# A decoder step on TensorE: the moving rows stored in two halves, every second token in the other half

## The chip, the core and the metric

The kernel runs on one core of one Trainium2 chip. The metric is the time in microseconds (us) that the device takes for one execution of the program; lower is better. Traces come from the hardware profiler, for one execution.

## The reference

One inference step of a hybrid decoder layer for two groups of requests that share all weights: a prompt of 256 tokens and 8 single-token samples, together 264 token columns. All data is float32, the model width is 2048. In short:

```python
def layer(x):
    proj = rms_norm(x, g_mix) @ w_in            # 2048 x 6688: q, k, v | z, xBC | dt
    attn = sliding_window_attention(q, k, v)    # 16 heads of 64, window 128, sinks
    ssd  = mamba2(z, conv4(xBC), dt)            # 32 heads of 64, state 128
    x = x + concat([attn, ssd]) @ w_out         # 3072 x 2048
    q = rms_norm(rms_norm(x, g_cross) @ w_cq)   # 4 heads of 128
    k, v = rms_norm(h @ w_ck), h @ w_cv         # h = rms_norm(memory, g_mem), 256 memory tokens
    x = x + softmax(q k / sqrt(128)) v @ w_co   # 512 x 2048
    u = conv3(rms_norm(x, g_ffn) @ w_up)        # 2048 x 11264
    return x + (silu(gate) * val) @ w_down      # 5632 x 2048
```

The samples use cached keys, values, memory and convolution rows in place of those of the prompt, and the step also returns the new caches and states.

## The kernel before, in words

Everything is kept transposed: features on the 128 partitions, tokens along the row. A matrix product takes a 128x128 block of weights as the stationary operand and a row of 264 tokens (256 prompt, 8 samples) as the moving one, and adds 264 output columns into a PSUM bank.

Precision is held by a split. Each float32 number is stored as two numbers of the type fp32r, a high part (the value rounded) and a low part (the rest). `weights` (L76) loads 1024 columns of weights at a time into `wraw`, ScalarE writes the high part `whi` (L89), VectorE the low part `wlo` (L90). `split` (L94) does the same for the tokens: ScalarE writes the high part, VectorE the low part (L97 without a gain, L98 and L99 with one). `mm3` (L104) then makes a block's product out of three: high weights with high tokens (L105), high weights with low tokens (L106), low weights with high tokens (L107). `proj` (L109) loops over weight units, the two or four output blocks and the blocks of the sum.

The split tokens lie in tiles that `rows` (L67) makes: 8 rows of a pitch of 320 numbers, of which 264 are used, each with token t at place t:

```python
PITCH = 320
    def rows(tag, name):
        return apool.tile([128, 8, PITCH], F32R, tag=tag, name=name, bufs=4)[:, :, :T]
```

These tiles are `A` (xh, xl: input of the layer, written by `x_hi` L165 and `x_lo` L169 in the opening), `Y` (yh, yl: the gated state-space output), `AT` (ath, atl: the attention output), `X1` (x1h, x1l), `OH` and `OL` (ohl: the cross-attention output), `X2` (x2h, x2l: the FFN's input) and `H` (hh, hl: the FFN's hidden rows). Some are written in two parts, the 256 prompt columns by one pair of instructions and the 8 sample columns by another.

In order of time: an opening in which the input and the first weights arrive and 192 products run (`first_k`, L242, to about 30 us); the input projection with convolutions, attention and the state-space scan between its products (to about 360 us); the output projection (to about 499 us); the cross-attention, in which memory keys (`keys`, L1159) and values (`v_pair`, L1280) are made the other way round, with the memory rows as stationary operand and the weights as the moving one, 512 columns for keys and 256 for values (to about 605 us); the FFN, 44 hidden blocks in six groups, up-projections of a group alternating with down-projections of the one before (to the end). The order of instructions on each engine is set by the tile framework's scheduler, with priorities and `issue_after` marks; the opening is ordered by hand. All weight loads are issued from SyncE's queue, and a load waits until VectorE has finished with the buffer. GpSimd issues some state loads and stores and does small elementwise work.

Of the kernel before, what the change touches and what calls it, by code (L numbers as in the profile page):

```python
# [48 lines left out]
def hybrid_decoder_step_kernel(ctx: ExitStack, tc: tile.TileContext, I, O):  # L49
# [17 lines left out]
    def rows(tag, name):  # L67
        return apool.tile([128, 8, PITCH], F32R, tag=tag, name=name, bufs=4)[:, :, :T]

# [24 lines left out]
    def split(hi, lo, x, g=None):  # L94

        if g is None:
            return S.copy(out=hi, in_=x), V.tensor_tensor(out=lo, in0=x, in1=hi.bitcast(F32), op=ALU.subtract)  # L97
        return (S.activation(out=hi, in_=x, func=AF.Copy, scale=g),  # L98
                V.scalar_tensor_tensor(out=lo, in0=x, scalar=g, in1=hi.bitcast(F32), op0=ALU.mult, op1=ALU.subtract))  # L99
# [9 lines left out]
    def proj(units, acts, evac, n=T, nb=2, tag="mm"):  # L109

        outs = [psum(t) for t in (tag if isinstance(tag, list) else [tag] * nb)]
        for ui, (src, act) in enumerate(zip(units, acts)):
            parts = src if isinstance(src, list) else weights(src)
            for pi, (wh, wl) in enumerate(parts):
                wh = wh.rearrange("p (k c) -> p k c", c=128 * nb)
                wl = wl.rearrange("p (k c) -> p k c", c=128 * nb)
                nk = wh.shape[1]
                for m in range(nb):
                    for k in range(nk):
                        kk = pi * nk + k  # L120
                        ah, al = act(8 * ui + kk) if callable(act) else (act[0][:, kk, :n], act[1][:, kk, :n])
                        last = mm3(outs[m][:, :n], wh[:, k, m * 128:(m + 1) * 128], wl[:, k, m * 128:(m + 1) * 128],
                            ah, al,
                            ui == 0 and kk == 0, ui == len(units) - 1 and kk == nk * len(parts) - 1)
                if ui == 0:
                    marks["part"] = last
        for m in range(nb):
            with tc.high_priority():
                evac(m, outs[m][:, :n])
# [35 lines left out]
    def x_hi(k):  # L165
        x, g = x_of(k)
        return S.activation(out=A[k // 8][0][:, k % 8, :], in_=x, func=AF.Copy, scale=g)

    def x_lo(k):  # L169
        x, g = x_of(k)  # L170
        return V.scalar_tensor_tensor(out=A[k // 8][1][:, k % 8, :], in0=x, scalar=g, in1=A[k // 8][0][:, k % 8, :].bitcast(F32),
                                      op0=ALU.mult, op1=ALU.subtract)
# [27 lines left out]
    with tc.manual_schedule(engines={mybir.EngineType.SP, mybir.EngineType.PE, mybir.EngineType.Activation, mybir.EngineType.DVE}):  # L200
# [41 lines left out]
        def first_k(k, i):  # L242

            for x in range(2 - i):
                for c in range(4):
                    PE.matmul(first[c][:, :T], pre[k // 2][i][:, k % 2, c * 128:(c + 1) * 128], A[k // 8][x][:, k % 8, :],  # L246
                              start=k + i + x == 0, stop=k == KB - 1 and i == 1)
# [698 lines left out]
    def z_pair(i):  # L946
# [9 lines left out]
        for m in range(2):  # L956
            k = 2 * i + m
            y = y2[:, m, :]
            sumsq(accy[:, :TP], y, k == 0, TP, V)
            split(Y[k // 8][0][:, k % 8, :TP], Y[k // 8][1][:, k % 8, :TP], y, gssd[:, k:k + 1])  # L960

    def gate_sample():
# [13 lines left out]
        for h in range(2):  # L976
            split(Y[h][0][:, :, TP:T], Y[h][1][:, :, TP:T], ysam[:, 8 * h:8 * h + 8, :])

# [32 lines left out]
    with tc.high_priority():  # L1011
        for j in (0, 4):
            split(AT[0][:, j:j + 4, :], AT[1][:, j:j + 4, :], attn[:, j:j + 4, :])
    w_out = I["w_out"]
# [66 lines left out]
    for i in range(8):  # L1081
        def ev(m, pm, i=i):
            k = 2 * i + m
            x = res[k // 4][:, k % 4, :]
            t = small.tile([128, T], F32, tag="raw", name="raw")
            V.tensor_tensor(out=t, in0=pm, in1=ry, op=ALU.mult)
            V.tensor_tensor(out=x, in0=t, in1=x, op=ALU.add)
            marks["x1"] = split(X1[k // 8][0][:, k % 8, :], X1[k // 8][1][:, k % 8, :], x, pc("g_cross", k))
        proj([w_out[8 + 2 * i], w_out[9 + 2 * i]], Y, ev, tag="t" if i % 2 else "mm")
# [69 lines left out]
    def keys():  # L1159
        pk = [psum("mm") for _ in range(2)]  # L1160
        for u in range(4):
            for pi, (wh, wl) in enumerate(weights(I["w_ck"][u])):
                wh, wl = (w.rearrange("p (k c) -> p k c", c=512) for w in (wh, wl))
                for k in range(2):
                    kk = 4 * u + 2 * pi + k
                    mhi, mlo = mem_hl(kk)
                    for c in range(2):
                        cs = slice(c * 128, c * 128 + 128)
                        mm3(pk[c], mhi[:, cs], mlo[:, cs], wh[:, k, :], wl[:, k, :], kk == 0, kk == KB - 1)
        ks = xp.tile([128, 2, 4], F32, name="ks")  # L1170
# [65 lines left out]
    def sample_out():  # L1236
# [14 lines left out]
        for q in range(2):  # L1251
            x = p[:, 0:128].rearrange("p (j c) -> p j c", j=4)[:, :, 4 * q:4 * q + 4].rearrange("p j m -> p m j")
            cs = slice(TP + 4 * q, TP + 4 * q + 4)
            split(OH[:, :, cs], OL[:, :, cs], x)
# [25 lines left out]
    def v_pair(i):  # L1280
        pv = [psum("mm") for _ in range(2)]
        for u in range(2):
            parts = [w.rearrange("p (k c) -> p k c", c=256) for hl in weights(I["w_cv"][2 * i + u]) for w in hl]
            nk = parts[0].shape[1]
            for k in range(8):
                wh, wl = parts[2 * (k // nk)], parts[2 * (k // nk) + 1]
                mhi, mlo = mem_hl(8 * u + k)
                for c in range(2):
                    cs = slice(c * 128, c * 128 + 128)
                    mm3(pv[c][:, 0:256], mhi[:, cs], mlo[:, cs], wh[:, k % nk, :], wl[:, k % nk, :],  # L1290
                        u + k == 0, u == 1 and k == 7)
# [3 lines left out]
    def out_head(h):  # L1295
# [4 lines left out]
        with tc.high_priority():  # L1300
            return split(OH[:, h, :TP], OL[:, h, :TP], o[:, 0:256])

# [22 lines left out]
    OHL = rows("A", "ohl")  # L1325
    OH, OL = OHL[:, 0:4, :], OHL[:, 4:8, :]
    lg = sample_logits()
# [19 lines left out]
    def x2_ev(k, pm):  # L1347
        x = res[k // 4][:, k % 4, :]
        V.tensor_tensor(out=x, in0=pm, in1=x, op=ALU.add)
        split(X2[k // 8][0][:, k % 8, :], X2[k // 8][1][:, k % 8, :], x, pc("g_ffn", k))  # L1350


    outs = [psum(t) for t in ("mm", "mm", "t", "t")]
    for pi, (wh, wl) in enumerate(weights(I["w_co"][0])):
        wh, wl = (w.rearrange("p (k c) -> p k c", c=512) for w in (wh, wl))
        for k in range(2):
            h = 2 * pi + k
            for m in range(4):
                ms = slice(m * 128, m * 128 + 128)
                mm3(outs[m][:, :T], wh[:, k, ms], wl[:, k, ms], OH[:, h, :], OL[:, h, :], h == 0, h == 3)  # L1360
    for m in range(4):
# [63 lines left out]
    def up(g):  # L1425
        H = (rows("A", f"hh{g}"), rows("A", f"hl{g}"))
        n = len(groups[g])
        for ii, i in enumerate(groups[g]):
# [27 lines left out]
            V.tensor_tensor(out=cs[1], in0=cs[0], in1=cs[1], op=ALU.mult)  # L1456
            split(H[0][:, ii, :TP], H[1][:, ii, :TP], cs[1])
        b0 = groups[g][0]
# [8 lines left out]
        V.tensor_tensor(out=sc[1], in0=sc[0], in1=sc[1], op=ALU.mult)  # L1467
        split(H[0][:, 0:n, TP:T], H[1][:, 0:n, TP:T], sc[1])
        return H
# [53 lines left out]
def _pack(np, x):  # L1523
# [129 lines left out]
```

## Time and profile before

| what | value |
|---|---|
| median of 3 runs | 1376.23 us (1375.93 to 1378.35) |
| profiled execution | 1375.38 us, span 1373.6 us |
| TensorE busy | 1368.6 us, 100% of the span, 11412 products and transposes |
| VectorE, ScalarE, GpSimd busy | 1045.0, 769.5, 90.8 us |
| HBM traffic | 216 GB/s over the span |
| granted TensorE clock | full in all slices |

The span runs from the first to the last instruction; the execution's own time has some 1.8 us around it. A TensorE row's duration reaches from its start to its modelled end and overlaps that of the next products, so the distance between two starts, and not the duration, says how long TensorE is held. "128*128 128x264" in such a row is the shape of the weights and of the moving operand; "x2h,whi" are the moving and the stationary tile, or the other way round where the name sorts so. Weight loads have rows of their own (PEld) and overlap the products.

### The profile page before, as it was taken

Reading aid. Unit: us, or ns where it says so; the run is one execution under the profiler, and the core shown is the slowest. Engines: PE = TensorE matmul, PEld = TensorE weight load, DVE = VectorE, ACT = ScalarE, POOL = GpSimd, SP = SyncE. Lnnn points to the kernel's source line nnn. Section 1 sums busy time; section 2 is a strip of 40 time slices with the busy share of each in tenths; the row PEclk is TensorE's granted clock in tenths of the full one; section 3 lists DMA queues with packets and bytes.
Section 4 is the critical chain, followed back from the end, with each engine's and each line's share of the span. In section 5 each row is a group of like instructions: output and inputs, shape, how many; then the busy total and the mean of one; then the engine's idle time right before and its main releaser. Section 6 shows DMA issues by size and latency. Waiting matters only on the chain.

```text
span 1373.6 us, 28651 instructions
## 1 busy us (share of the span) xinstructions
PE 1368.6 (100%) x11412; PEld 1347.2 (98%) x11412; DVE 1045.0 (76%) x1797; ACT 769.5 (56%) x1253; POOL 90.8 (7%) x284
## 2 busy tenths in 40 slices
PE   9999999999999999999999999999999999999998
PEld 9999999999999999899999999999999999999998
DVE  8979899999987774488777765776577657765655
ACT  7667776855546545475566644554455446544532
POOL 0000101111100000002110000000000000000000
PEclk9999999999999999999999999999999999999999
DMA  7954588667786576675676765676567556655554
GB/s 304 329 158 150 174 281 261 196 212 229 243 262 210 182 244 221 259 268 190 197 248 220 251 219 179 221 255 216 184 215 246 196 187 198 198 180 185 194 185 137
DMA packets 88326, 298.31 MB, mean 217 GB/s; under 512 B 11905, under 2 KB 17025, under 8 KB 87681
## 3 DMA queue, kind: packets, MB, share of 16 engines
q1 hardware_dynamic: 82688, 277.61, 60.9%
q0 software_dynamic: 5504, 18.88, 4.2%
q8 instruction: 89, 1.46, 0.4%
q14 instruction: 45, 0.36, 0.1%
HBM read 280.77 MB, written 16.23 MB: 216 GB/s over the span
## 4 chain that ended last, share of the span: by engine, by line
PE 100%; DVE 0%; ACT 0%; issue 0%
PE mm L107 21%; PE mm L105 21%; PE mm L106 21%; PE t L107 10%; PE t L106 10%; PE t L105 10%; PE t L246 1%; PE t L284 1%; PE x L866 1%; PE mm L246 0%; PE s L246 0%; PE x L284 0%; PE s L875 0%; PE t L569 0%; PE x L1198 0%; PE x L1242 0%
## 5 line engine op out<-in xcount | busy, mean ns | idle before, releaser
L89 ACT CAST whi<-wraw 128x1024 fp32r<-128x1024 f32 x440 | 460.4, 1048 | 531.1 <-PE mm L106 279.2
L90 DVE TENSOR_TENSOR wlo<-wraw,whi 128x1024 fp32r<-128x1024 f32 x440 | 541.9, 1233 | 218.3 <-ACT whi L89 212.0
L107 PE MATMUL t<-x2h,wlo 128*128 128x264 f32 x704 | 198.6, 282 | 0.0
L106 PE MATMUL t<-x2l,whi 128*128 128x264 f32 x704 | 198.4, 282 | 0.0
L105 PE MATMUL t<-x2h,whi 128*128 128x264 f32 x704 | 198.4, 282 | 0.0
L106 PE MATMUL mm<-hl,whi 128*128 128x264 f32 x704 | 197.6, 282 | 0.0
L107 PE MATMUL mm<-hh,wlo 128*128 128x264 f32 x704 | 197.3, 282 | 0.0
L105 PE MATMUL mm<-hh,whi 128*128 128x264 f32 x704 | 195.7, 282 | 0.0
L105 PE MATMUL mm<-x2h,whi 128*128 128x264 f32 x672 | 189.4, 282 | 0.0
L106 PE MATMUL mm<-x2l,whi 128*128 128x264 f32 x672 | 189.4, 282 | 0.0
L107 PE MATMUL mm<-x2h,wlo 128*128 128x264 f32 x672 | 189.4, 282 | 0.0
L107 PE MATMUL mm<-xh,wlo 128*128 128x264 f32 x576 | 164.4, 287 | 0.0
L106 PE MATMUL mm<-xl,whi 128*128 128x264 f32 x576 | 163.3, 284 | 0.0
L105 PE MATMUL mm<-xh,whi 128*128 128x264 f32 x576 | 163.3, 285 | 0.0
L107 PEld LDWEIGHTS t<-x2h,wlo 128*128 128x128 f32 x704 | 131.9, 187 | 0.0
L105 PEld LDWEIGHTS t<-x2h,whi 128*128 128x128 f32 x704 | 131.9, 187 | 0.0
L106 PEld LDWEIGHTS t<-x2l,whi 128*128 128x128 f32 x704 | 131.9, 187 | 0.0
L106 PEld LDWEIGHTS mm<-hl,whi 128*128 128x128 f32 x704 | 131.9, 187 | 0.0
L107 PEld LDWEIGHTS mm<-hh,wlo 128*128 128x128 f32 x704 | 131.7, 187 | 0.0
L105 PEld LDWEIGHTS mm<-hh,whi 128*128 128x128 f32 x704 | 130.8, 187 | 0.0
L105 PEld LDWEIGHTS mm<-x2h,whi 128*128 128x128 f32 x672 | 125.9, 187 | 0.0
L106 PEld LDWEIGHTS mm<-x2l,whi 128*128 128x128 f32 x672 | 125.9, 187 | 0.0
(522 smaller groups left out, 2933.4 us busy)
## 6 DMA issues: line engine op xcount, KB each, us to landing
wraw<-in_w_up_dram SPq DMA_DIRECT2D x176, 512.0 KB, 4.1
wraw<-in_w_in_dram SPq DMA_DIRECT2D x96, 512.0 KB, 4.4
wraw<-in_w_dn_dram SPq DMA_DIRECT2D x88, 512.0 KB, 4.2
wraw<-in_w_out_dram SPq DMA_DIRECT2D x48, 512.0 KB, 4.5
h<-in_h_dram POOLq DMA_DIRECT2D x32, 256.0 KB, 4.7
hn<-in_h_dram SPq DMA_DIRECT2D x16, 512.0 KB, 4.9
out_state_s_dram<-hn POOLq DMA_DIRECT2D x16, 512.0 KB, 3.3
late<-dram_la SPq DMA_DIRECT2D x8, 512.0 KB, 6.8
```

The lines of the kernel that those rows point to most:

```text
L89: highs.append(S.copy(out=hi, in_=x))
L90: lows.append(V.tensor_tensor(out=lo, in0=x, in1=hi.bitcast(F32), op=ALU.subtract))
L105: PE.matmul(out, wh, xh, start=start, stop=False)
L106: PE.matmul(out, wh, xl, start=False, stop=False)
L107: return PE.matmul(out, wl, xh, start=False, stop=stop)
L246: PE.matmul(first[c][:, :T], pre[k // 2][i][:, k % 2, c * 128:(c + 1) * 128], A[k // 8][x][:, k % 8, :], start=k + i + x == 0, stop=k == K ...
L284: return PE.transpose(out, in_, cst[0:k, C_ID:C_ID + k])
L866: PE.matmul(st, Bn[:, c, g, :], sts[c].rearrange("p h q -> p (h q)"), start=True, stop=True)
```

## The change

The rows of split tokens keep their pitch and their 264 places, but token t = 2b + a now lies at place 132 a + b: even tokens fill the first half, odd tokens the second. The view that `rows` returns has the two dimensions b (132, step 1) and a (2, step 132), so whoever goes through it in order meets the tokens in their natural order, reading or writing the two halves in turn. `split`, `x_hi` and `x_lo` write through this view (their input is viewed as pairs), the products read through it, and the output columns in PSUM are in natural order as before. Prompt columns are the pairs 0 to 127, sample columns the pairs 128 to 131.

The key and value weights, which are the moving operand of the memory's products, are permuted on the host (`apart`): in each group of 512 (keys) or 256 (values) columns the even columns come first. The products read them through the same kind of view, halves 256 and 128 numbers apart. No instruction, transfer or wait is added or taken away. The products of the attention's own keys (kh, kl), the plain float32 products and the transposes stay as they are.

```diff
     def rows(tag, name):
-        return apool.tile([128, 8, PITCH], F32R, tag=tag, name=name, bufs=4)[:, :, :T]
+        return apool.tile([128, 8, PITCH], F32R, tag=tag, name=name, bufs=4)[:, :, :T].rearrange("p k (a b) -> p k b a", a=2)
+
+    PROMPT, SAMPLES = slice(0, TP // 2), slice(TP // 2, T // 2)
+
+    def pairs(x):
+
+        if len(x.shape) == 2:
+            return x.rearrange("p (b a) -> p b a", a=2)
+        return x.rearrange("p k (b a) -> p k b a", a=2)
...
     def split(hi, lo, x, g=None):
 
+        if len(hi.shape) > len(x.shape):
+            x = pairs(x)
...
-                        ah, al = act(8 * ui + kk) if callable(act) else (act[0][:, kk, :n], act[1][:, kk, :n])
+                        ah, al = act[0][:, kk], act[1][:, kk]
...
-        return S.activation(out=A[k // 8][0][:, k % 8, :], in_=x, func=AF.Copy, scale=g)
+        return S.activation(out=A[k // 8][0][:, k % 8], in_=pairs(x), func=AF.Copy, scale=g)
...
-            split(Y[k // 8][0][:, k % 8, :TP], Y[k // 8][1][:, k % 8, :TP], y, gssd[:, k:k + 1])
+            split(Y[k // 8][0][:, k % 8, PROMPT], Y[k // 8][1][:, k % 8, PROMPT], y, gssd[:, k:k + 1])
...
-                wh, wl = (w.rearrange("p (k c) -> p k c", c=512) for w in (wh, wl))
+                wh, wl = (w.rearrange("p (k a b) -> p k b a", k=2, a=2) for w in (wh, wl))
...
-            parts = [w.rearrange("p (k c) -> p k c", c=256) for hl in weights(I["w_cv"][2 * i + u]) for w in hl]
+            parts = [w.rearrange("p (k a b) -> p k b a", a=2, b=128) for hl in weights(I["w_cv"][2 * i + u]) for w in hl]
...
-            split(H[0][:, ii, :TP], H[1][:, ii, :TP], cs[1])
+            split(H[0][:, ii, PROMPT], H[1][:, ii, PROMPT], cs[1])
...
+    def apart(w, c):
+
+        return w.reshape(w.shape[0], -1, c // 2, 2).swapaxes(2, 3).reshape(w.shape)
...
-    d["w_ck"] = units(x["w_ck"][0], 4, 512)
-    d["w_cv"] = units(x["w_cv"][0], 8, 256)
+    d["w_ck"] = units(apart(x["w_ck"][0], 512), 4, 512)
+    d["w_cv"] = units(apart(x["w_cv"][0], 256), 8, 256)
```

More of the change, by code (lines that the diff above doesn't have):

```diff
@@ L166, in x_hi @@
         x, g = x_of(k)
-        return S.activation(out=A[k // 8][0][:, k % 8, :], in_=x, func=AF.Copy, scale=g)
+        return S.activation(out=A[k // 8][0][:, k % 8], in_=pairs(x), func=AF.Copy, scale=g)
     def x_lo(k):
         x, g = x_of(k)
-        return V.scalar_tensor_tensor(out=A[k // 8][1][:, k % 8, :], in0=x, scalar=g, in1=A[k // 8][0][:, k % 8, :].bitcast(F32),
+        return V.scalar_tensor_tensor(out=A[k // 8][1][:, k % 8], in0=pairs(x), scalar=g, in1=A[k // 8][0][:, k % 8].bitcast(F32),
                                       op0=ALU.mult, op1=ALU.subtract)
@@ L245, in first_k @@
                 for c in range(4):
-                    PE.matmul(first[c][:, :T], pre[k // 2][i][:, k % 2, c * 128:(c + 1) * 128], A[k // 8][x][:, k % 8, :],
+                    PE.matmul(first[c][:, :T], pre[k // 2][i][:, k % 2, c * 128:(c + 1) * 128], A[k // 8][x][:, k % 8],
                               start=k + i + x == 0, stop=k == KB - 1 and i == 1)
@@ L976, in gate_sample @@
         for h in range(2):
-            split(Y[h][0][:, :, TP:T], Y[h][1][:, :, TP:T], ysam[:, 8 * h:8 * h + 8, :])
+            split(Y[h][0][:, :, SAMPLES], Y[h][1][:, :, SAMPLES], ysam[:, 8 * h:8 * h + 8, :])
     res = []
@@ L1012, in hybrid_decoder_step_kernel @@
         for j in (0, 4):
-            split(AT[0][:, j:j + 4, :], AT[1][:, j:j + 4, :], attn[:, j:j + 4, :])
+            split(AT[0][:, j:j + 4], AT[1][:, j:j + 4], attn[:, j:j + 4, :])
     w_out = I["w_out"]
@@ L1087, in ev @@
             V.tensor_tensor(out=x, in0=t, in1=x, op=ALU.add)
-            marks["x1"] = split(X1[k // 8][0][:, k % 8, :], X1[k // 8][1][:, k % 8, :], x, pc("g_cross", k))
+            marks["x1"] = split(X1[k // 8][0][:, k % 8], X1[k // 8][1][:, k % 8], x, pc("g_cross", k))
         proj([w_out[8 + 2 * i], w_out[9 + 2 * i]], Y, ev, tag="t" if i % 2 else "mm")
@@ L1168, in keys @@
                         cs = slice(c * 128, c * 128 + 128)
-                        mm3(pk[c], mhi[:, cs], mlo[:, cs], wh[:, k, :], wl[:, k, :], kk == 0, kk == KB - 1)
+                        mm3(pk[c], mhi[:, cs], mlo[:, cs], wh[:, k], wl[:, k], kk == 0, kk == KB - 1)
         ks = xp.tile([128, 2, 4], F32, name="ks")
@@ L1252, in sample_out @@
             x = p[:, 0:128].rearrange("p (j c) -> p j c", j=4)[:, :, 4 * q:4 * q + 4].rearrange("p j m -> p m j")
-            cs = slice(TP + 4 * q, TP + 4 * q + 4)
+            cs = slice(TP // 2 + 2 * q, TP // 2 + 2 * q + 2)
             split(OH[:, :, cs], OL[:, :, cs], x)
@@ L1289, in v_pair @@
                     cs = slice(c * 128, c * 128 + 128)
-                    mm3(pv[c][:, 0:256], mhi[:, cs], mlo[:, cs], wh[:, k % nk, :], wl[:, k % nk, :],
+                    mm3(pv[c][:, 0:256], mhi[:, cs], mlo[:, cs], wh[:, k % nk], wl[:, k % nk],
                         u + k == 0, u == 1 and k == 7)
@@ L1300, in out_head @@
         with tc.high_priority():
-            return split(OH[:, h, :TP], OL[:, h, :TP], o[:, 0:256])
+            return split(OH[:, h, PROMPT], OL[:, h, PROMPT], o[:, 0:256])
     keys()
@@ L1325, in hybrid_decoder_step_kernel @@
     OHL = rows("A", "ohl")
-    OH, OL = OHL[:, 0:4, :], OHL[:, 4:8, :]
+    OH, OL = OHL[:, 0:4], OHL[:, 4:8]
     lg = sample_logits()
@@ L1349, in x2_ev @@
         V.tensor_tensor(out=x, in0=pm, in1=x, op=ALU.add)
-        split(X2[k // 8][0][:, k % 8, :], X2[k // 8][1][:, k % 8, :], x, pc("g_ffn", k))
+        split(X2[k // 8][0][:, k % 8], X2[k // 8][1][:, k % 8], x, pc("g_ffn", k))
     outs = [psum(t) for t in ("mm", "mm", "t", "t")]
@@ L1359, in hybrid_decoder_step_kernel @@
                 ms = slice(m * 128, m * 128 + 128)
-                mm3(outs[m][:, :T], wh[:, k, ms], wl[:, k, ms], OH[:, h, :], OL[:, h, :], h == 0, h == 3)
+                mm3(outs[m][:, :T], wh[:, k, ms], wl[:, k, ms], OH[:, h], OL[:, h], h == 0, h == 3)
     for m in range(4):
@@ L1467, in up @@
         V.tensor_tensor(out=sc[1], in0=sc[0], in1=sc[1], op=ALU.mult)
-        split(H[0][:, 0:n, TP:T], H[1][:, 0:n, TP:T], sc[1])
+        split(H[0][:, 0:n, SAMPLES], H[1][:, 0:n, SAMPLES], sc[1])
         return H
```

## The prediction

> **What bounds the kernel now.** I read the page first: busy shares, granted clock, chain of work that ended last.
>
> ```profile
> span 1373.6 us, 28651 instructions
> PE 1368.6 (100%) x11412; PEld 1347.2 (98%) x11412; DVE 1045.0 (76%) x1797; ACT 769.5 (56%) x1253; POOL 90.8 (7%) x284
> PEclk9999999999999999999999999999999999999999
> PE 100%; DVE 0%; ACT 0%; issue 0%
> ```
>
> TensorE is never without work, its clock is granted in full in every slice, and the chain that sets the end is TensorE all the way. So the only thing worth pricing first is how long one product holds TensorE. A matmul row's own duration (282 ns in the groups) does not say that, because products overlap in the pipeline; the distance from one start to the next does. I took the starts from the timeline: a stretch of the FFN (264 columns moving), of the value products (256), of the key products (512), and two plain-float32 products. Columns: start us, duration us, line, output<-inputs, weight and moving shapes, count.
>
> ```profile
> 700.07 0.28 PE L107 MATMUL t<-x2h,wlo 128*128 128x264 f32 x1
> 700.19 0.28 PE L105 MATMUL t<-x2h,whi 128*128 128x264 f32 x1
> ...
> 714.83 0.28 PE L107 MATMUL t<-x2h,wlo 128*128 128x264 f32 x1
> ...
> 556.08 0.28 PE L107 MATMUL mm<-whi,ml 128*128 128x256 f32 x1
> ...
> 558.46 0.28 PE L107 MATMUL mm<-whi,ml 128*128 128x256 f32 x1
> ...
> 581.18 0.28 PE L107 MATMUL mm<-whi,ml 128*128 128x256 f32 x1
> ...
> 582.60 0.28 PE L107 MATMUL mm<-whi,ml 128*128 128x256 f32 x1
> ...
> 499.92 0.40 PE L107 MATMUL mm<-whi,ml 128*128 128x512 f32 x1
> ...
> 520.92 0.40 PE L107 MATMUL mm<-whi,ml 128*128 128x512 f32 x1
> ...
> 209.86 1.02 PE L866 MATMUL x<-xw,Bn 128*128 128x512 f32 x2
> ...
> 561.19 1.03 PE L1260 MATMUL y<-qk 128*128 128x256 f32 x4
> ...
> L866 PE MATMUL x<-xw,Bn x16: 590/592/697, 209.9 to 315.8; 128*128 128x512 f32 x16
> ...
> L1260 PE MATMUL y<-qk x8: 379/379/382, 561.2 to 569.6; 128*128 128x256 f32 x8
> ```
>
> 264 columns: 14.76 us hold 123 steps, 120.0 ns each. 256 columns: 2.38 us over 21 steps, 113.3 ns; later, with other buffers, 1.42 us over 12 steps, 118.3 ns. 512 columns: 21.00 us over 90 steps, 233.3 ns. Plain float32 runs in two passes at a lower rate: 512 columns take 1.02 - 0.59 = 0.43 us from one start to the next, 256 take (1.03 - 0.379) / 3 = 217 ns, so (430 - 217) / 256 = 0.83 ns a column. If the fp32r rate is just twice that, 0.416 ns a column, the streams alone would need 106.5, 110 and 213 ns for 256, 264 and 512 columns. That the ratio is two is an estimate; the measured fp32r steps lie 7, 10 and 20 ns above it. The float32 products carry only about 4 ns beside their columns (217 - 256 x 0.83). So the fp32r stream has an excess of its own which grows with the columns read, and for one shape is 113.3 at one place and 118.3 at another: it behaves like a cost of reading the moving operand at the full rate, not like a fixed cost of an instruction. The change touches exactly the order of that read.
>
> **The change part by part.**
>
> It adds and removes no instruction, byte or wait. (1) The split rows keep 264 columns, but token 2b+a lies at a x 132 + b, so each product reads from two places 528 bytes apart in turn and still writes its output columns in order. (2) The writes of these rows by ScalarE and VectorE alternate likewise. (3) The key and value weights are permuted on the host, so their splitting stays as it is, and the product reads halves 1024 and 512 bytes apart. I price (1) by stages; the counts are those of one of the three products (L105), hence times three.
>
> ```profile
> core 0: us, PE busy (x) PEld busy (x), PEclk, DMA share, GB/s
> 30.60:210.00 179.40, 117.90 (x416) 77.72 (x416) 1.00 0.68 219
> 210.00:330.00 120.00, 77.33 (x270) 50.72 (x271) 1.00 0.69 223
> 330.00:360.00 30.00, 23.51 (x85) 15.67 (x85) 1.00 0.71 229
> 360.00:499.00 139.00, 108.28 (x384) 71.76 (x383) 1.00 0.67 218
> 499.00:605.00 106.00, 63.14 (x214) 39.63 (x213) 1.00 0.74 265
> 605.00:1370.00 765.00, 595.23 (x2123) 396.33 (x2123) 1.00 0.63 205
> ...
> core 0: us, PE busy (x) PEld busy (x) DVE busy (x) ACT busy (x) POOL busy (x), PEclk, DMA share, GB/s
> 0.00:30.60 30.60, 29.40 (x233) 27.65 (x234) 24.33 (x39) 25.36 (x39) 0.28 (x6) 1.00 0.80 312
> 210.00:330.00 120.00, 120.00 (x1024) 114.93 (x1023) 117.48 (x197) 76.44 (x138) 20.09 (x26) 1.00 0.69 223
> 605.00:1370.00 765.00, 764.95 (x6373) 764.67 (x6372) 538.30 (x870) 390.77 (x590) 54.54 (x216) 1.00 0.63 205
> ```
>
> The price of an alternating moving read is in no row: every moving operand of this trace is contiguous. From below it is bounded by the 110 ns estimate (10 ns less a product), from above by the float32 rate: 264 x 0.83 + 4 = 223 ns (103 ns more). Between these far ends I take the row nearest in kind, the 256-column product at 113.3 ns: same fp32r stream, same weight loads, the least excess seen. It is also the shortest step at which the trace shows a 128-column weight load per product keeping up, and the weight load is what would be late next. So 6.7 ns less for each 264-column product.
>
> FFN, 605 to 1370 us: 3 x 2123 = 6369 products, 42.5 us. Output projection, 360 to 499: 1152, 7.7 us. Between 499 and 605, 214 less the 96 that belong to keys and values, times three, 354: 2.4 us. The 96 key products of 512 columns: 233.3 to 2 x 113.3, 0.6 us. The value products: nothing. Input projection outside 210 to 330: 3 x (416 + 85) = 1503, 10.0 us. Inside it 810 products would give 5.4 us, but VectorE is busy 117.48 of 120 us there, so I grant only its idle 2.5 us. In the FFN VectorE has 227 us to spare and ScalarE 374, and DMA is at 0.63; a 6% faster TensorE is still fed. The opening's 192 products (16 rows, 4 column blocks, 3 products each) could give 1.3 us. Sum: 67.0 us.
>
> (2) costs time where the writing engine is on the path. No row writes alternating single elements; the nearest reads them: a reduction over 128 elements that lie 32 bytes apart, beside the same 128 elements in order.
>
> ```profile
> L974 DVE TENSOR_REDUCE accy<-ts 128x8 f32<-128x128 f32 x1 | 0.4, 405 | 0.0
> L973 DVE TENSOR_TENSOR ts<-ysam 128x128 f32<-128x128 f32 x1 | 0.3, 284 | 0.0
> ...
> L99 DVE SCALAR_TENSOR_TENSOR yl<-xs,gssd,yh 128x256 fp32r<-128x256 f32 x16 | 8.0, 533 | 0.0
> L171 DVE SCALAR_TENSOR_TENSOR xl<-open,open,xh 128x264 fp32r<-128x264 f32 x12 | 5.5, 491 | 0.7 <-ACT xh L167 0.6
> ```
>
> 121 ns more for 128 elements, 0.95 ns each. At that price a split row of 264 costs 0.25 us more on each engine: 16 rows in the opening, 4.0 us, where ScalarE is busy 25.36 of 30.6 us, and some 9 of the 16 yl rows fall before 330 us, 2.2 us on VectorE without slack. So (2) costs between nothing and 6 us (a gain is excluded: the same elements are written). I take 2 us, since the row is a read, and a reduction that starts eight times. In the FFN 44 such rows would add 11 us to an engine with 227 us idle: nothing. After the change of order, the last split before a stage's first product (the x2 rows at 613 us) is exposed by at most 0.25 us.
>
> 67.0 - 2 = 65. The profiled execution took 1375.38 us (span 1373.6 and 1.8 around it), 0.85 below the median 1376.23. So 1310.4 for it, 1311 against the median.
>
> On the rate, the Trainium skill's page "TensorE: Matmul & The Clock Gate", section "Back-to-back issue gap", gives columns / 2.4 + 2.5 ns, which is 112.5 ns for 264 columns; that is an estimate from the page, by which the sum would be some 8 us larger. This trace disagrees with it for the contiguous fp32r read (120.0 measured).
>
> **The rivals.**
>
> A, no change: 1376 us. From 256 to 264 columns the step grows by 6.7 ns, although 8 columns are 3.3 ns at the 0.416 rate; so the excess may come in lumps tied to the length, about 16 columns' time (16 x 0.416 = 6.7), whatever the order. Against it: the same 256 columns at 113.3 and at 118.3.
>
> B, slower by one lump: if the read fetches pieces of 16 elements (the lump just named) and pays for each piece it touches, the 264 columns touch 17 if the row begins on one; two halves of 132, the second beginning a quarter into a piece, touch 9 each, 18. One lump more, 126.7 ns; the 10380 products counted above x 6.7 = 69 us, no cover on TensorE: 1445 us. The step to 118.3 for the same length shows that the start of a read can cost most of a lump. It decides as soon as a product takes over 120 ns.
>
> C, much slower: if every element that leaves its neighbour costs a fetch, the stream falls to the float32 rate, 223 ns: 10380 x 103 ns = 1069 us more, about 2445. The reduction above, which pays 0.95 ns for each distant element, speaks for it; against it, two lines held open would serve four elements each, as a contiguous read does. The Trainium skill speaks for C as well: "Advanced Engine Details and Errata", section "SBUF Cachelines", asks for at least two hits on a 16-byte line and names a penalty where every access takes another line. The reduction's row agrees with that on VectorE; no run here shows it on TensorE.
>
> **How the numbers follow.** Faster as forecast 0.62: the excess scales with columns read and moves with the buffer, which is what a read-order cost looks like, and everything else in the long FFN stage has slack. A 0.13, B 0.13, C 0.12. The likeliest case's own range: at 110 ns, 63.7 + 11.5 + 3.5 + 15.0 + 2.5 + 1.9 + 1.3 = 99 us less, 1277; and a partial cure at 113.3 / 256 x 264 = 116.9 ns, about 31 us less, 1345. The whole range takes in A and B, and leaves out C: 1280 to 1450, which holds some 0.85. A measurement of this kernel tells about 0.2% from no change; faster 0.62, same 0.13, slower 0.25.
>
> **What would show it.** Right: the 264-column products start about 113 ns apart in the FFN with the clock still full, the span shrinks mostly after 605 us, and the stage from 210 to 330 us shrinks least while VectorE shows almost no idle time. The key products fall to about 227 ns. (2) right: yl and xl rows stay near 533 and 491 ns. A: steps of 120.0 ns again. B: 126.7. C: 200 ns or more, with VectorE and ScalarE idle far more. The prediction is wrong if the excess belongs to the weight loads or to the length; then steps stay, or a new step appears that does not depend on the halves' distance (528, 1024, 512 bytes).

## The result: about 1311.5 us, 4.8% less time

Three executions of the changed kernel took 1308.13 to 1312.20 us, with 1311.46 in the middle (a fourth took 3500.39 us, was disturbed, and is left out of the comparison); the kernel before took 1376.08 beside them: ratio 0.952, 95% interval 0.950 to 0.955. The profiled execution took 1311.46 us with a span of 1309.7, where 1373.6 stood before. The order of the instructions on each engine is the same in both traces, so every difference below is one of durations and waits.

The page of the changed kernel, first line, TensorE's row and the chain that ended last:

```profile
span 1309.7 us, 28651 instructions
PE 1294.7 (99%) x11412; PEld 1272.1 (97%) x11412; DVE 1061.0 (81%) x1797; ACT 793.6 (61%) x1253; POOL 94.8 (7%) x284
PE 82%; DVE 8%; DMA 5%; issue 2%; ACT 2%; SPq 0%; DVEq 0%; ACTq 0%; POOLq 0%
```

TensorE lost 73.9 us of busy time, the span 63.9. The rest shows in the chain: TensorE is no longer all of it, 8% are VectorE's and 5% transfers. The next fence is the timeline of the changed kernel: first products of the stages, and two stretches whose steps can be counted (columns as in the prediction).

```profile
31.68 0.47 PE L115 MATMUL mm<-xh,whi 128*128 128x264 f32 x1
...
353.68 0.39 PE L115 MATMUL mm<-ath,whi 128*128 128x264 f32 x2
...
485.85 0.28 PE L117 MATMUL t<-yh,wlo 128*128 128x264 f32 x1
485.96 0.38 PE L115 MATMUL mm<-whi,mh 128*128 128x512 f32 x1
...
506.46 0.38 PE L117 MATMUL mm<-whi,ml 128*128 128x512 f32 x1
...
588.50 0.28 PE L115 MATMUL s<-x2h,whi 128*128 128x264 f32 x1
...
654.81 0.28 PE L115 MATMUL t<-x2h,whi 128*128 128x264 f32 x1
...
671.91 0.28 PE L117 MATMUL t<-x2h,wlo 128*128 128x264 f32 x1
```

264 columns: 17.10 us over 152 steps, 112.5 ns each (120.0 before). 512 columns: 20.50 us over 95 steps, 215.8 ns (233.3 before). The Trainium skill's page "TensorE: Matmul & The Clock Gate", section "Back-to-back issue gap", gives columns / 2.4 + 2.5 ns as the gap of a single product taken by itself, that is 112.5 and 215.8, and about 131 ns for 512 columns in a stream of products with their weight loads. This trace is such a stream: its read in turn agrees to a tenth with the gap of the single product and not with the 131, and the read in order, before, agreed with neither.

The same four stage marks in the trace of the kernel before:

```profile
30.66 0.48 PE L105 MATMUL mm<-xh,whi 128*128 128x264 f32 x1
...
359.60 0.40 PE L105 MATMUL mm<-ath,whi 128*128 128x264 f32 x2
...
498.64 0.28 PE L107 MATMUL t<-yh,wlo 128*128 128x264 f32 x1
...
605.18 0.28 PE L105 MATMUL s<-x2h,whi 128*128 128x264 f32 x1
```

The differences of neighbouring marks give the stages, the last one reaching to the end of the span. The two columns on the right are two experiments told below (reading in turn with the old storage; storage in halves written half by half), from the same four marks of their traces.

| stage, us | before | after | change | predicted | read alone | halves written in order |
|---|---|---|---|---|---|---|
| opening | 30.7 | 31.7 | +1.0 | +2.7 | 30.2 | 30.7 |
| input projection | 328.9 | 322.0 | -6.9 | -12.5 | 320.9 | 319.5 |
| output projection | 139.0 | 132.2 | -6.9 | -7.7 | 130.4 | 130.4 |
| cross-attention | 106.5 | 102.7 | -3.9 | -3.0 | 102.3 | 102.3 |
| FFN to the end | 768.4 | 721.2 | -47.2 | -42.5 | 720.7 | 720.7 |
| sum | 1373.6 | 1309.7 | -63.9 | -63.0 | 1304.4 | 1303.5 |

"Predicted" counts the opening as 4.0 us for its writes less 1.3 for its products, the prediction's own single prices; its sum took 2 us for all the writes together and came to -65.0. The other side of the change, the split rows of the changed kernel (groups by form):

```profile
L107 DVE TENSOR_TENSOR hl<-c,hh 128x256 fp32r<-128x256 f32 x44 | 27.5, 626 | 0.0
...
L181 DVE SCALAR_TENSOR_TENSOR xl<-open,open,xh 128x264 fp32r<-128x264 f32 x12 | 7.6, 707 | 0.6 <-ACT xh L177 0.5
...
L107 DVE TENSOR_TENSOR atl<-attn,ath 128x1056 fp32r<-128x1056 f32 x2 | 4.2, 2210 | 0.0
```

xl took 491 ns before, 707 now: 216 ns more for 264 elements, 0.82 ns each, close to the 0.95 of the strided reduction that the prediction took as its bound and then set aside. On ScalarE xh went from 506 to 764 ns, 0.98 ns an element.

### The profile page after: what moved, and what is told of

Same layout as the page of the kernel before. It is cut to its first block, busy times and chain, and to the rows that moved or that the text cites. A ratio compares the mean times of both kernels' runs of the same rounds, so it can differ in the third digit from the quotient of the medians.

```text
span 1309.7 us, 28651 instructions
## 1 busy us (share of the span) xinstructions
PE 1294.7 (99%) x11412; PEld 1272.1 (97%) x11412; DVE 1061.0 (81%) x1797; ACT 793.6 (61%) x1253; POOL 94.8 (7%) x284
## 4 chain that ended last, share of the span: by engine, by line
PE 82%; DVE 8%; DMA 5%; issue 2%; ACT 2%; SPq 0%; DVEq 0%; ACTq 0%; POOLq 0%
PE mm L115 17%; PE mm L117 17%; PE mm L116 17%; PE t L115 9%; PE t L116 9%; PE t L117 9%; DVE wlo L98 3%; DMA wraw<-in_w_in_dram 1%; DMA open<-in_open_dram 1%; DMA kt<-in_mk_dram 1%; DMA wraw<-in_w_co_dram 1%; DVE c L781 1%; ACT whi L97 1%; DMA cpast<-in_cpast_dram 0%; DMA cb<-dram_bc 0%
## 5 line engine op out<-in xcount | busy, mean ns | idle before, releaser
L117 PE MATMUL t<-x2h,wlo 128*128 128x264 f32 x704 | 194.5, 276 | 0.0
L116 PE MATMUL t<-x2l,whi 128*128 128x264 f32 x704 | 194.3, 276 | 0.0
L115 PE MATMUL t<-x2h,whi 128*128 128x264 f32 x704 | 194.3, 276 | 0.0
L116 PE MATMUL mm<-hl,whi 128*128 128x264 f32 x704 | 193.3, 276 | 0.0
L117 PE MATMUL mm<-hh,wlo 128*128 128x264 f32 x704 | 193.0, 276 | 0.0
L115 PE MATMUL mm<-hh,whi 128*128 128x264 f32 x704 | 191.5, 276 | 0.0
L116 PE MATMUL mm<-x2l,whi 128*128 128x264 f32 x672 | 185.5, 276 | 0.0
L117 PE MATMUL mm<-x2h,wlo 128*128 128x264 f32 x672 | 185.5, 276 | 0.0
L115 PE MATMUL mm<-x2h,whi 128*128 128x264 f32 x672 | 185.5, 276 | 0.0
L117 PE MATMUL mm<-xh,wlo 128*128 128x264 f32 x576 | 161.4, 282 | 0.0
```

Of the source, the lines that this page charges most:

```text
L115: PE.matmul(out, wh, xh, start=start, stop=False)
L116: PE.matmul(out, wh, xl, start=False, stop=False)
L117: return PE.matmul(out, wl, xh, start=False, stop=stop)
```

## The experiments

The theory to test: a product that reads its moving fp32r operand in order pays for two neighbouring numbers out of the same small piece of memory; two places in turn spare it that, and nothing else of the change helps. Its rivals: the two places must be far apart; or the storage, and not the reading, helps; or the length alone sets the step.

### One step per pattern, measured alone

A kernel of its own: 48 products in a row for each pattern, with eight 128x128 weights in rotation, no other work. It computes nothing of the layer.

```diff
+    def halves(n, d):    # two places d numbers apart, in turn
+        return M[:, 0:2 * d].rearrange("p (a d) -> p a d", a=2)[:, :, 0:n // 2].rearrange("p a b -> p b a")
+    def runs(n, r):      # r from one half, r from the other
+        return M[:, 0:n].rearrange("p (a b r) -> p b a r", a=2, r=r)
+    for i, (name, n, mv) in enumerate(tests):
+        for j in range(48):
+            PE.matmul(bank(i, name)[:, :n], W[:, 128 * (j % 8):128 * (j % 8) + 128], mv, start=j == 0, stop=j == 47)
```

> A kernel of its own: nothing of the layer is computed; 48 products of 128x128 fp32r weights for each read pattern of the moving operand, alone on the chip, then ScalarE and VectorE splits with several write patterns. Theory 1, the order of the read decides (a contiguous fp32r read pays for its single line after line, two lines in turn do not): 264 columns in order 120 ns from start to start, in halves 112.5; 512 columns 233 and 216; the excess in order grows with the columns; runs of 2 or 4 tokens from each half cure it too if only different lines in turn are wanted, and any distance between the halves does. Theory 2, two far places are wanted (separate parts of the memory): halves 16 or 48 bytes apart stay at 120, only distances from some hundreds of bytes give 112.5. Theory 3, the 112.5 is now the weight load's limit and not the columns': with halves, 240 and 256 columns take 112 too, and the step falls no further with fewer columns. If the columns set it, 240 take about 102 and 192 about 82. bfloat16 in order, 264 columns: 112.5 under all (no excess for 2-byte elements). Writes: a split of 264 in halves takes about 0.77 us on ScalarE and 0.70 on VectorE against 0.50 and 0.43 in order; runs of four somewhere between.

Its first sweep over the columns ran in part at half the granted clock (45.5 to 62.5 us and 144.4 to 161.5 us of its span); the second such kernel, below, repeats it. The patterns that follow ran at the full clock. Timeline of TensorE, 48 products to a row: a step is the distance from one row's start to the next row's start, over 48.

```profile
346.29 5.56 PE L112 MATMUL disti<-mov,wts 128*128 128x264 f32 x48
351.69 5.56 PE L112 MATMUL nearfour<-mov,wts 128*128 128x264 f32 x48
...
373.29 8.32 PE L112 MATMUL runtwo<-mov,wts 128*128 128x264 f32 x48
...
399.44 7.03 PE L112 MATMUL partfour<-mov,wts 128*128 128x264 f32 x48
...
424.54 11.70 PE L112 MATMUL steptwo<-mov,wts 128*128 128x264 f32 x48
```

Two places 2048 numbers apart (disti) and two places 4 numbers apart (nearfour) take the same 112.5 ns; so did every distance between that was tried. Places that must be far apart fall as a theory. Other orders are worse than in order: two numbers from each half in turn 170 ns (the row after runtwo starts at 381.45), four from each 127, four parts in turn 143 (the next row starts at 406.31), every second number 240 (436.06), every fourth 240 as well. That runs of two and four would cure the read too, as theory 1 had it, is refuted. The rival C of the prediction is real, but it starts one step away from what this change does. The same run read 264 columns in order from starts 1 to 32 numbers further on: 120 to 126 ns, and 256 columns 117 to 123 ns. So the step in order depends on where the row starts as well; no simple rule of the start shows. Writing was measured beside it (groups, ScalarE, 264 columns):

```profile
L131 ACT CAST whalvesh<-raw 128x264 fp32r<-128x264 f32 x6 | 4.0, 674 | 0.2
...
L131 ACT CAST wruntwoh<-raw 128x264 fp32r<-128x264 f32 x6 | 2.6, 438 | 0.2
...
L131 ACT CAST wcontigh<-raw 128x264 fp32r<-128x264 f32 x6 | 2.5, 410 | 0.2
```

A write that takes the halves in turn costs 264 ns more, one that takes two numbers in each half 28 more. Reading and writing want opposite orders.

### Reading in turn without the storage

The kernel before, its products reading the two halves of rows that are stored in order. Tokens and output columns no longer agree, so it does not compute the layer; the work is the same.

```diff
+    def turn(x):
+        return x.rearrange("p (a b) -> p b a", a=2)
-    ... (act[0][:, kk, :n], act[1][:, kk, :n])
+    ... (turn(act[0][:, kk, :n]), turn(act[1][:, kk, :n]))
```

and the same at the opening's products, the keys, the values and the cross-attention's output.

> Rows and memory weights stored in order, as before the change, but the products read the two halves in turn; the output columns of these products come out in another order, so the tokens are mixed up from there on, at the same work. Theory 1 (the read's order decides): 112.5 ns a product, and the writes cost what they did before (yl 533 ns, xl 491 ns), so it is faster than the changed kernel by what the alternating writes cost there: opening about 2 us, input projection about 5 us: 1303 to 1308 us. Rival (the place of the tokens matters, not the order of the read): 120 ns, 1376 us.

1305.87 us, ratio 0.949 (0.948 to 0.951), span 1304.4. Timeline of the FFN, and the opening's splits (groups):

```profile
699.73 0.28 PE L107 MATMUL mm<-x2h,wlo 128*128 128x264 f32 x1
...
715.93 0.28 PE L107 MATMUL t<-x2h,wlo 128*128 128x264 f32 x1
```

```profile
L174 DVE SCALAR_TENSOR_TENSOR xl<-open,open,xh 128x264 fp32r<-128x264 f32 x12 | 5.5, 490 | 0.7 <-ACT xh L170 0.6
```

16.20 us over 144 steps, 112.5 ns, with xl as short as before (of the rows, yl alone is longer, 577 ns for 533). The reading order alone makes the whole gain; the change's span is 5.3 us longer than this one, and what differs is the writes.

### The storage without reading in turn

The changed kernel, its products going through the stored rows half after half, again with columns out of their order.

```diff
+    def straight(x):
+        return x.rearrange("p b a -> p a b")
-    ah, al = act[0][:, kk], act[1][:, kk]
+    ah, al = straight(act[0][:, kk]), straight(act[1][:, kk])
```

> Rows and memory weights stored in halves as in the changed kernel, but the products read them in order; again the tokens come out mixed up, at the same work. Theory 1: 120 ns a product as before, ScalarE splits 0.77 us and VectorE splits 0.70 us; TensorE hides nearly all of it: 1377 to 1382 us. Rival (storage alone cures the read): 112.5 ns, 1312 us.

1376.39 us, ratio 1.0005 (0.9996 to 1.0015). Timeline of the FFN:

```profile
699.74 0.28 PE L115 MATMUL t<-x2h,whi 128*128 128x264 f32 x1
...
715.93 0.28 PE L115 MATMUL mm<-x2h,whi 128*128 128x264 f32 x1
```

135 steps in 16.19 us, 119.9 ns. Storage without the reading order brings nothing. The slow writes (hl 615 ns here) cost at most 2 us (1.0015 x 1376) while TensorE runs at its old pace, less than expected. The 5.3 us beside the reading run are thus not a fixed price: they come up when the faster TensorE uses up the slack that covers them.

### Key and value weights back in order

```diff
-    wh, wl = (w.rearrange("p (k a b) -> p k b a", k=2, a=2) for w in (wh, wl))
+    wh, wl = (w.rearrange("p (k c) -> p k c", c=512) for w in (wh, wl))
-    d["w_ck"] = units(apart(x["w_ck"][0], 512), 4, 512)
+    d["w_ck"] = units(x["w_ck"][0], 4, 512)
```

and the value weights likewise.

> The changed kernel with the key and value weights in order again. Theory 1: 96 key products go from 216 back to 233 ns, 1.7 us, 192 value products from 112 back to 113 to 118 ns, up to 0.8 us: 1313 to 1315 us. Rival (the memory products are hidden behind other work): 1312 us.

1311.34 us, ratio 0.9535 (0.9521 to 0.9549), against 0.9521 (0.9498 to 0.9545) of the change. Timeline of the key products:

```profile
485.63 0.39 PE L115 MATMUL mm<-whi,mh 128*128 128x512 f32 x1
...
504.30 0.40 PE L117 MATMUL mm<-whi,ml 128*128 128x512 f32 x1
```

18.67 us over 80 steps are back at 233.4 ns, so the keys' share is 96 x 17.5 = 1.7 us. In this trace the cross-attention takes 105.0 us (482.01 to 586.99), 2.3 more than with the change; the 0.6 beside the keys stand at the value products, which the prediction had put at nothing. It is seen in the steps; the comparison of times, whose intervals overlap, cannot tell it, and the 1313 to 1315 us that were expected did not come.

One more thing can be read from this run. Up to the memory's products its kernel is the changed kernel, with the same instructions in the same order. Yet its trace has 31.1 us for the opening and 318.8 for the input projection, where the changed kernel's has 31.7 and 322.0. The input projection of one and the same kernel thus differs by 3.2 us between two executions, while the output projection (132.1) and the FFN (721.2) agree to 0.1.

### Near orders and other lengths

The second kernel of single patterns, with each length in order and in turn side by side.

```diff
+    for n in (264, 256, 512, 384, 320, 288, 240, 224):
+        tests.append(("order" + NAMES[n], n, M[:, 0:n]))
+        tests.append(("turn" + NAMES[n], n, halves(n)))
+    for name, d in (("neartwo", 2), ("nearthree", 3), ("nearfour", 4), ("nearsix", 6)):
+        tests.append((name, 264, M[:, 0:264].rearrange("p (c a b) -> p c b a", a=2, b=d)))
```

> A kernel of its own again, nothing of the layer computed: 48 products for each read pattern. 'order' reads a row of 224 to 512 columns in order, 'turn' in halves; 'near' reads two places 2, 3, 4 or 6 elements apart in turn; 'pairsswapped' reads 1, 0, 3, 2 and so on. Theory 1a (what cures the read is that two neighbouring reads never take the same 16-byte line one after the other): places 2 elements apart lie half the time in one line, so 'neartwo' and 'pairsswapped' stay near 120 or get worse, as runs of two did (171). Theory 1b (what costs is a step of exactly one element after another; any order that never makes two steps of +1 in a row is cured): 'neartwo', 'nearthree', 'nearsix' take 112.5 and 'pairsswapped' too. Floor: if the columns set the step in turn, 224, 240 and 256 take 95.8, 102.5 and 109.2 (2.4 columns a ns and 2.5 ns); if the weight load does, all three stay at 111 to 112. Writes: pairs swapped and places 2 apart on ScalarE and VectorE between 0.43 (in order) and 0.68 us (halves).

Timeline, 48 products to a row:

```profile
31.58 5.92 PE L113 MATMUL orderf<-mov,wts 128*128 128x264 f32 x48
37.34 5.56 PE L113 MATMUL turnf<-mov,wts 128*128 128x264 f32 x48
...
53.84 11.06 PE L113 MATMUL orderj<-mov,wts 128*128 128x512 f32 x48
64.74 10.52 PE L113 MATMUL turnj<-mov,wts 128*128 128x512 f32 x48
...
117.01 5.52 PE L113 MATMUL orderd<-mov,wts 128*128 128x240 f32 x48
122.37 5.52 PE L113 MATMUL turnd<-mov,wts 128*128 128x240 f32 x48
...
150.10 5.99 PE L113 MATMUL neartwo<-mov,wts 128*128 128x264 f32 x48
155.93 6.88 PE L113 MATMUL nearthree<-mov,wts 128*128 128x264 f32 x48
162.65 5.57 PE L113 MATMUL nearfour<-mov,wts 128*128 128x264 f32 x48
```

In order 120.0 ns. In turn between places 2 numbers apart: 121.5 ns, no gain; neighbours swapped (1, 0, 3, 2) took 121.3. 3 apart: 140.0, a loss. 4 apart (16 bytes): 112.5, the whole gain, and 6 apart the same. So neighbouring reads have to leave the 16 bytes they are in, and two such lines in turn are enough. Leaving them is not enough by itself, as the four parts (143) and every fourth number (240) show. At 240 columns both orders take 111.5 to 111.7 ns, and 192 and 128 columns took 111.3 to 111.7 as well: at full clock no product with a 128x128 weight followed the one before it sooner, whatever it read. The 264 columns read in turn, at 112.5, stand about 0.8 ns above that floor. In the first kernel of patterns 64 columns took 111 to 112 ns, and 64, 128 and 192 columns all took 213 to 214 ns where the clock was half: the floor knows nothing of the columns. One more row of this run, a group of VectorE: a split that reads every second number and writes in order.

```profile
L136 DVE TENSOR_TENSOR wreadhalvesl<-raw,wreadhalvesh 128x264 fp32r<-128x264 f32 x6 | 2.6, 432 | 0.2
```

ScalarE's row of the same kind takes 430; all in order they take 432 and 411, writing the halves in turn 621 and 669. The dear part of a split into halves is the jumping write; the jumping read costs 20 ns at most. That suggested a version that is told further below.

### Less work for VectorE in the input projection

Both kernels without the multiplication and the sum of the samples' state scan; `ych` is set to zero, so the samples' scan output is left out.

```diff
-    V.tensor_tensor(out=h0, in0=h0, in1=held[2 * g + q], op=ALU.mult)
-    V.tensor_reduce(out=ych[:, 4 * g + i, rows], in_=h0, op=ALU.add, axis=AX.X)
```

The changed kernel so cut:

> The changed kernel without the multiplication and the reduction of the samples' cached states (32 pairs of VectorE instructions, 44 us of VectorE's time between 190 and 400 us); the sample outputs lack that term. Theory (VectorE is what holds the input projection back after the change): TensorE's idle time there goes and the stage shrinks by up to 10 us: 1301 to 1306 us. Rival (the stage is held by loads or by ScalarE): 1311 us.

The kernel before so cut:

> The same work left out of the kernel before. Theory: TensorE was never idle in that stage, so nothing is gained: 1374 to 1377 us. Rival (VectorE held the stage already before): 1366 to 1370 us.

1316.18 us (ratio to the kernel before 0.9565, 0.9550 to 0.9579) and 1384.43 us (1.0063, 1.0047 to 1.0080). Both are slower than with the work in, which no theory had. The reason is that the scheduler, given fewer instructions, laid the stage out anew (616 of TensorE's 11412 places hold another instruction, in both pairs). In the trace of the cut changed kernel TensorE idles 12.5 us in the input projection, 5.1 more than in the changed kernel's, and three of its waits (2.7, 2.4 and 5.5 us) are each followed by 3.4 us at a granted clock of 0.50; the last section comes back to this. The longest wait of TensorE between 200 and 320 us in the cut changed kernel is one that the changed kernel does not have:

```profile
PE x L294 <- DVE cnew L774: 5.5, 1, 5.5
```

So these two runs decide nothing on VectorE.

### The halves written one after the other

The changed kernel, storage and reading kept, but each split goes through its row half by half: it writes in order and reads every second token. It computes the same layer.

```diff
+    def flip(x):
+        return x.rearrange("p b a -> p a b" if len(x.shape) == 3 else "p k b a -> p k a b")
     if len(hi.shape) > len(x.shape):
-        x = pairs(x)
+        hi, lo, x = flip(hi), flip(lo), flip(pairs(x))
```

and `x_hi`, `x_lo` likewise.

> The changed kernel, but the splits write each half from end to end and read every second token of their input instead (same places, same products, same results). Theory (the 0.2 to 0.3 us that a split lost is the alternating write): splits take 0.50 us on ScalarE and 0.49 on VectorE again, and the time is that of the kernel whose reads alone alternate: 1303 to 1308 us. Rival (a read with a step costs the engines as much as the alternating write): 1310 to 1313 us.

1303.45 us (1302.80 to 1305.33), ratio 0.9474 (0.9461 to 0.9487): faster than both kernels, its interval apart from that of the change. Groups:

```profile
L184 DVE SCALAR_TENSOR_TENSOR xl<-open,open,xh 128x264 fp32r<-128x264 f32 x12 | 5.5, 490 | 0.7 <-ACT xh L180 0.7
```

xl is as short as before the change, and so are the other rows but yl (580 ns, as in the reading run). The difference of the ratios, 0.0047 x 1376 = 6.5 us, and that of the spans, 1309.7 - 1303.5 = 6.2 us, are what the jumping writes cost here.

### Places 16 bytes apart, and runs of two, in the whole kernel

The reading run again with other orders.

```diff
-        return x.rearrange("p (a b) -> p b a", a=2)
+        return x.rearrange("p (c a b) -> p c b a", a=2, b=4)        # places 4 numbers apart
+        return x.rearrange("p (a b r) -> p b a r", a=2, r=2)        # two from each half
```

> As the kernel whose reads alone alternate (tokens come out mixed up, same work), but the two places that a product reads in turn are 4 elements, 16 bytes, apart in place of 528 bytes (memory weights likewise). Theory 1a (two neighbouring reads in different 16-byte lines, any distance): 112.5 ns a product, 1304 to 1308 us. Theory 2 (far places are wanted): 120 ns, 1370 us or more.

> As the kernel whose reads alone alternate, but two tokens from the first half, then two from the second, and so on. By the patterns measured alone (171 ns for 264 columns): 59 ns more for each of some 10380 products than in turns of one, 1900 to 1925 us. Rival (the pattern costs less where weights change and other engines work): under 1500 us.

4 numbers apart: 1304.25 us, ratio 0.9478 (0.9461 to 0.9496), with steps of 112.5 ns; the distance is without effect in the kernel too. Runs of two: 1917.86 us. Timeline of its FFN:

```profile
999.69 0.35 PE L107 MATMUL mm<-x2h,wlo 128*128 128x264 f32 x1
...
1019.83 0.35 PE L105 MATMUL t<-x2h,whi 128*128 128x264 f32 x1
```

20.14 us over 118 steps, 170.7 ns. Rows written two numbers at a time, which costs a split next to nothing, and read in that order would have cost 542 us.

## Why the prediction was right

**The bound and the mechanism.** TensorE's step was the bound, and the excess of the fp32r stream is a cost of the order of reading: reading in turn alone gives 0.949, storage alone 1.0005. Rival A (no change, excess tied to the length) is refuted by steps of 120.0 and 112.5 ns for the same 264 columns; B (126.7 ns) by the same rows. C's price does not fall on two lines in turn, but the prediction's doubt was sound: every second number takes 240 ns. The Trainium skill's page "Advanced Engine Details and Errata", section "SBUF Cachelines", foresees a penalty where every access takes another line; the 112.5 ns of two lines in turn disagree, the 143 ns of four parts and the 240 ns of every fourth number agree. It asks for two hits on a line; runs of two (170 ns) and every second number (240 ns) take two numbers of a line one after the other and are dear all the same, so here the trace disagrees again. What the chip does inside these reads stays open; shown is which orders are cheap.

**The step that was mis-sized: 113.3 ns.** The prediction took the 256-column product as its nearest price. That product read in order too, so it was no price for a read in turn, only a value that lay near: 112.5 was measured. 6369 FFN products x 0.8 = 5.1 us, and the FFN gave 47.2 where 42.5 were forecast. The keys gave 17.5 ns a product in place of 6.7 for the same reason. The low bound of 110 ns cannot be had: some 111 ns is the least that any length took. That the weight load sets this floor, as the prediction named it next in line, fits 64 to 240 columns at one step, but was not separated from other fixed costs.

**The step that failed in place: the input projection.** 1503 + 810 = 2313 products x 7.5 ns could have given 17.3 us, 12.5 were forecast, 6.9 came. The prediction looked for the loss where VectorE was full, 210 to 330 us. The windows of the changed kernel show it at three places (columns: window, length, PE, PEld, DVE, ACT, POOL busy, clock, DMA share, GB/s); before, TensorE was busy in every one of these to the last hundredth.

```profile
60.00:80.00 20.00, 17.84 (x142) 17.48 (x141) 15.89 (x27) 9.44 (x14) 1.10 (x2) 0.91 0.71 257
...
160.00:200.00 40.00, 38.25 (x398) 37.24 (x397) 35.40 (x78) 28.05 (x50) 4.29 (x8) 1.00 0.88 280
...
200.00:240.00 40.00, 38.99 (x344) 37.01 (x343) 40.00 (x69) 26.76 (x50) 6.51 (x7) 1.00 0.78 252
...
280.00:320.00 40.00, 38.38 (x346) 36.15 (x343) 40.00 (x60) 20.44 (x31) 9.32 (x9) 1.00 0.60 197
```

From 200 to 320 us VectorE is full, as foreseen, and TensorE idles 1.0 + 0.9 + 1.6 = 3.5 us (240 to 280, not shown, has 39.13), all of it in waits for VectorE's tiles hp (2.6) and xw (0.9). But 2.2 us are lost at 60 to 80 and 1.8 at 160 to 200, where VectorE has time to spare. The chain of the changed kernel at the first of them (start us, duration us, what):

```profile
60.84 7.79 DMA wraw<-in_w_in_dram
68.73 1.05 ACT whi L97
69.81 1.23 DVE wlo L98
...
71.36 0.35 DVE attn L425
```

A load of weights takes 7.8 us, ScalarE and VectorE split it, and an attention step queued behind that split on VectorE comes late. TensorE's timeline there:

```profile
71.76 0.59 PE L115 MATMUL mm<-xh,whi 128*128 128x264 f32 x1 [2.16 <-DVE attn L425]
...
75.18 0.28 PE L115 MATMUL mm<-xh,whi 128*128 128x264 f32 x1
```

And the wait has an echo: after it the products step by 220 ns until 75.18 (granted clock 0.91 over the window of 20 us, 0.50 from 71.80 to 75.10), 15 of them in 3.42 us, where 15 x 0.1125 = 1.69 would do, 1.7 us more. 0.3 + 2.2 + 1.8 + 3.5 us of idle time between 30 and 320 us (0.3 at 30 to 60) and 1.7 of slow clock make 9.5 of the missing 10.4 us.

Not all of this belongs to the change. In the run with the key and value weights in order, whose kernel is the same up to there, the product at this place waited less and the clock stayed full. Its timeline:

```profile
70.12 0.38 PE L115 MATMUL mm<-xh,whi 128*128 128x264 f32 x1 [0.64 <-DVE attn L425]
```

Its load of weights took 6.3 us where it took 7.8, and its input projection came out 10.1 us shorter than before the change, not 6.9. So about 3 of the missing 10.4 us, the longer wait and its echo, came in one execution and not in the other; the 3.5 us at VectorE and most of the wait at 160 to 200 (1.2 us there) are in both. The wait at 160 to 200 stands behind a transfer too; from the waits of that window (total us, times, longest):

```profile
DVE h L939 <- DMA cb<-dram_bc: 3.7, 1, 3.7
...
PE s L725 <- DVE zz L719: 1.7, 1, 1.7
```

VectorE waits for a broadcast that goes through memory, and the step that TensorE wants (zz) comes after it in VectorE's queue. "A faster TensorE is still fed" was examined for the FFN, where it held, and not for this stage. Between the products that started at 210 and 330 us before the change, 1.7 us were gained where the prediction granted 2.5; in the rest of the stage, 5.2 where it counted the full 10.0 (in the trace with the memory weights in order, 1.7 and 8.4). That the VectorE part would go with less work on VectorE stays open, since the two runs meant for it changed the layout.

**The writes.** Right in kind, wrong in the value chosen: between the bounds of 0 and 6 us the prediction took 2, since the row was a reduction. The elements cost 0.82 ns on VectorE and 0.98 on ScalarE, about the bound's 0.95, and 5 to 6.5 us were paid by the two comparisons. By the table, against the reading run: 1.5 in the opening, 1.1 in the input projection, 1.8 in the output projection, 0.3 and 0.5 later; the 1.1 is less than the 3.2 us by which two executions differ in that stage, and so is not shown to be the writes'. The 1.8 were not in the prediction at all: the attention's rows (ath, atl) are written as 1056 elements at once, 2.2 us on each engine, and TensorE waits 0.7 us for the last of them, which with its restart makes 1.0 of the 1.8; the rest are three later pauses, whose cause stays open. The claim that yl and xl "stay near 533 and 491 ns" failed, and the FFN's 44 rows, 27.5 us on VectorE in place of 18.3 in the reading run, are hidden whole. The FFN's 0.5 us stand at one product that waits 0.24 us for x2l, the exposed last split that the prediction had allowed 0.25 us.

**Why the sum came out all the same.** Against the 67.0 us of the products, the FFN and the cross-attention gave 5.6 more, the input projection 5.6 less, the output projection 0.8 less, and the opening lost 1.0 where 1.3 were to be gained: 63.9, with all writes in it. The prediction had 65.0, after 2 for the writes. Two errors of opposite sign, the product's price and the cover of the input projection with the writes, stand behind an agreement within about 1 us. That nearness is luck: the price of 113.3 came from a read of another kind, and the profiled execution lost about 3 us that another one did not. The direction and the mechanism are not luck.

## What to carry to other kernels

Where a trace shows back-to-back products slower than their columns, ask what order the moving operand is read in: two 16-byte lines in turn can be had by storage in halves, and a view is all that the product needs. Pay for the new layout on the side where it is cheap: on these engines the strided read of a split cost 20 ns at most and the strided write 190 to 270. When the bound engine becomes 6% faster, price every stage by its own cover, transfers and waiting queues included: in the stage with the least slack only 40% of the possible gain came in one execution, 58% in another.

## What the runs showed of the hardware that was not expected

- An fp32r product of 264 columns took 120 to 126 ns when it read in order, by where the row started, and 112.4 to 112.6 in turn between two places at any distance from 4 to 2048 numbers; 512 columns took 227 to 233 and 215.8. The step in order wandered for the same read (120.0, and 122.6 later in the same run), the step in turn did not. Why, and why the 256 columns of the kernel before took 113.3 in order at one place while 117 to 123 were measured alone, stays open.
- More than two places in turn are worse again: four 143 ns, six 153, eight 227; and so are two numbers from each of two places (170) and every second number (240).
- A bf16 product of 264 columns, read in order, took 112.6 ns: the excess was seen with fp32r alone.
- With a new 128x128 fp32r weight for each product, 64 to 240 columns all took 111 to 112 ns at full clock.
- Single numbers written in turn into two places 16 bytes or more apart cost ScalarE 669 to 684 ns for 264 where 410 are needed in order, VectorE 620 to 629 for 432; two numbers at a time, or places 2 apart, cost at most 28 ns more.
- A wait of 2.2 us between two products was followed by 3.4 us at half the pace, and so were, in the trace of the changed kernel with less scan work, waits of 2.4, 2.7 and 5.5 us; in that of the kernel before with less scan work a wait of 3.8 us went with 6.8 us at half the clock. None of the nineteen waits of 1.0 to 1.75 us within the ten traces of whole kernels had this echo.
